# Bias tiles of a two-layer mixer trunk read backwards from reversed rows, without shifted copies in DRAM

## The chip, the core and the metric

The kernel runs on one core of one Trainium2 chip. The metric is the device time of one execution in microseconds (us); a version's time is the median of its runs. The profile shows one execution of the kernel, engine by engine: PE is TensorE, DVE VectorE, ACT ScalarE, POOL GpSimd, and SP the SyncE queue, which here issues nearly all DMAs. Names with a q (SPq) are an engine's instruction queue.

## The reference

Two layers over 512 tokens of width 1024. Each layer normalises x, projects it, runs four attention branches, gates them, projects the outputs back and adds them to x. One table `rel_bias` of 32 buckets and 40 heads gives the relative-position biases of three branches; this is the part that the change touches:

```python
def t5_bucket(dist):                      # distance -> bucket 0..31
    ...
def band_bias(table, step):
    rel = BLOCK + jnp.arange(BLOCK)[:, None] - jnp.arange(2 * BLOCK)[None, :]
    return table[t5_bucket(rel * step)].transpose(2, 0, 1)

# banded_attention (branches B and D): bias (heads, 128, 256), the same for each block of 128 queries
s = jnp.einsum('bnqkgd,bnskd->bnkgqs', qb, kb) * dh ** -0.5
s = s + bias.reshape(hkv, g, BLOCK, 2 * BLOCK)
mask = (rel >= 0)[None] & (rel <= max_dist)[None] & key_ok
s = jnp.where(mask[None, :, None, None], s, -jnp.inf)
# dsa_attention (branch A): the 128 best keys of an indexer
bias = bias_table[t5_bucket(qpos[None, :, None] - idx)]
...
for l in range(DEPTH):
    xn = rms_norm(x, norm_gain[l])
    (A's, B's, C's, D's parts), gates = combined_projection(xn, w_in[l])
    ...
    merged = sum(sigmoid(gates[n]) * ((ys[n] * silu(zs[n])) @ w_branch[l, n]) for n in range(4))
    x = x + merged @ w_out[l]
```

A bias depends on query minus key alone. So the tile of a head, 128 queries by n keys, holds in each row the row above it shifted by one element.

## The kernel before

All products are fp32, made of three TensorE passes over a high and a low part of each operand. A layer runs through a list of jobs (`PLAN`): the indexer; then the branches in the order D, C, B, A, each a row of projection jobs and of attentions, one pair of heads at a time; the merges of a finished branch lie between the jobs of the next; a last group of merges, and the output projection. In the listing `idx`, `cin`, `pair`, `z`, `attD`, `attB` and so on are such jobs. A scheduler of the tile framework, which simulates a timeline, sets the order of each engine's instructions from the jobs' order, from what each needs, and from which buffers are free.

**Weights.** They stream from DRAM (`wall`) through `next_slot`. A slot is loaded by a DMA on SP (L402, `cbuf<-wall`) into one of four raw buffers, ACT casts the high part (L405), DVE subtracts to get the low part (L411), and PE reads both. A load waits on SP for the raw buffer that the subtraction of four slots earlier frees; everything behind it on SP waits with it. SP's DMAs use eight semaphores in turn, so a DMA also waits until the one eight before it has landed.

**Bias rows.** In layer 0 after the indexer, `later_consts` multiplies a one-hot matrix (made on the host by `bias_onehot`: for each position of a segment the bucket of its distance) with the bias table (PE, L335). The result, 41 rows (heads, and one causal row for branch C) by 1920 positions, is written to the DRAM tile `gdram` in four chunks of 480 columns (DVE copy to `th`, then L338). A row holds five segments: A of 640 positions, D 384, and the groups G0 384, G1 256, G2 256 of branch B.

**Shifted copies.** `make_skew` copies a segment of one pair of heads 128 times from `gdram` into another DRAM tile (`skew..`, L347). There are 21 such DMAs: one of 320 KB for C, eight of 384 KB, four of 640 KB and eight of 256 KB, all in layer 0. Their leading dimension is the pair of rows (2), the next the 128 copies with step 0. `load_bias` (L364 to L373) then reads a bias tile on SP (L372) with a step of w - 1 elements per partition, so that the row of partition i is shifted by i. `next_skew` asks for the next copies at certain jobs; `load_bias` does where none are there yet.

**Readers of a bias tile.** DVE adds the bias to the scores and takes the row minimum of the negated sum (L942); for pairs of score parts DVE first adds the bias to the second part (L940, L974); POOL adds the top-k mask in branch A (L934).

**Two other things that the prediction speaks of.** The latent projections of branch C transpose normed rows on PE (L803), from rows `PT` that DVE scales (L796) after ACT has copied a bank of PSUM to `raw` (L642). In branch B the row maxima and denominators of the groups with stride go through a small DRAM tile: `sd<-st` (L1183) and `nat<-sd` (L1185), both on SP, the second waiting for the first to land. PE's L1026 are the products of the probabilities with the values, whose transposed probabilities `PT` come from ACT (L547) and DVE (L548). POOL issues `U<-U` (L701, L702), which swaps halves of the keys.

Of the kernel before, what the change touches and what calls it, by code (L numbers as in the profile page):

```python
# [9 lines left out]
F32 = mybir.dt.float32  # L10
# [6 lines left out]
PSUM = bass.MemoryType.PSUM  # L17
# [5 lines left out]
NT = S // 128  # L23
# [14 lines left out]
SEG_A, SEG_D, SEG_G0, SEG_G1, SEG_G2 = 0, 640, 1024, 1408, 1664  # L38
SEG_LEN = 1920
SEG_ROWS = {SEG_A: (0, 8), SEG_D: (32, 8), SEG_G0: (8, 8), SEG_G1: (16, 8), SEG_G2: (24, 8)}  # L40
# [42 lines left out]
def job_slots(job):  # L83
    """Per weight slot: a list of (source, rows of 128, columns)."""
    kind = job[0]
    if kind in ("idx", "cin", "pair", "d0", "d1"):
        c = chunk_cols(job)
        return [[("w_in", 2 * i + j, c) for j in range(2)] for i in range(4)]
    if kind == "z":
        c = Z_OFF[job[1]] + job[2] * 128 + np.arange(128)  # L90
        return [[("w_in", 4 * i + j, c) for j in range(4)] for i in range(2)]
    if kind == "merge":
        n, ft = job[1], job[2]
        c = OFF_G + n * D + ft * 128 + np.arange(128)
        f = ft * 128 + np.arange(128)
        return [[("w_in", j, c) for j in range(6)],
                [("w_in", j, c) for j in (6, 7)] + [(("w_branch", n), j, f) for j in range(4)]]
    if kind == "out":
        f = job[1] * 128 + np.arange(128)
        return [[("w_out", 4 * i + j, f) for j in range(4)] for i in range(2)]  # L100
    if kind == "cq":
        q = job[1] * 384 + np.arange(384)
        return [[("w_q_b", 0, q), ("w_q_b", 1, q)]]
    if kind == "ckv":
        p = job[1]
        h = np.arange(64)
        kv = np.concatenate([(2 * p) * 128 + h, (2 * p + 1) * 128 + h,
                             (2 * p) * 128 + 64 + h, (2 * p + 1) * 128 + 64 + h])
        return [[("w_kv_b", 0, kv)]]
    raise ValueError(kind)  # L110


def plan():
    """The order of a layer's work; what comes first is preferred where several pieces are ready."""
    w = [("idx",)]
    merges = []

    def fill(n):
        for _ in range(min(n, len(merges))):
            m = merges.pop(0)  # L120
            w.append(m)

    for i, br in enumerate(ORDER):
        n = iter(FILL[i])
        if br == BR_D:
            w += [("d0",), ("d1",)]
            if i < 3 and ORDER[i + 1] == BR_C and CIN_AT < 0:
                w += [("cin",)]
        if br == BR_C and ("cin",) not in w:
            w += [("cin",)]  # L130
        if br == BR_A and ("topk",) not in w:
            w += [("topk",)]
        for p in range(4):
            if br == BR_B:
                for g in range(3):
                    w += [("pair", br, p, g), ("attB", p, g)]
                    if g == Z_AT:
                        w += [("z", br, p)]
                    fill(next(n))
                w += [("mix", p)]  # L140
                continue
            if br == BR_D:
                w += [("z", br, p), ("attD", p)]
            elif br == BR_A:
                w += [("pair", br, p), ("z", br, p), ("attA", p)]
            else:
                if p % 2 == 0:
                    w += [("cq", p // 2)]
                w += [("ckv", p), ("z", br, p), ("attC", p)]
            fill(next(n))  # L150
            w += [("y", br, p)]
            if i < 3 and ORDER[i + 1] == BR_C and p == CIN_AT:
                w += [("cin",)]
        if i < 3:
            merges += [("merge", br, j) for j in range(8)]
    fill(len(merges))
    w += [("merge", ORDER[3], i) for i in range(8)]
    w += [("split",)]
    w += [("out", i) for i in range(8)]
    return w  # L160
# [43 lines left out]
def bias_onehot():  # L204
# [7 lines left out]
    u = np.arange(640)  # L212
    seg(SEG_A, 640, 511 - u, 511 - u >= 0)
    u = np.arange(384)
    seg(SEG_D, 384, 255 - u, (255 - u >= 0) & (255 - u <= 127))
    seg(SEG_G0, 384, 255 - u, (255 - u >= 0) & (255 - u <= 128))
    u = np.arange(256)
# [24 lines left out]
def build(ctx, tc, A, depth=2, dump=None):  # L242
# [68 lines left out]
    skew = {}  # L311
# [28 lines left out]
    def make_skew(seg, r):  # L340
        """Rows r and r + 1 of a segment, 128 copies each, so that a load can shift copy i by i."""
        r0, nr = (C_ROW, 1) if seg == "C" else (SEG_ROWS[seg][0] + r, 2)
        o = SEG_A if seg == "C" else seg
        w = SEG_W[o]
        d = dp.tile([nr, 128, w], F32, name=f"skew{seg}_{r}")
        g = gdram[r0:r0 + nr, o:o + w]
        sy.dma_start(d, bass.AP(tensor=g.tensor, offset=g.offset, ap=[[SEG_LEN, nr], [0, 128], [1, w]]))  # L347
        for i in range(nr):
            skew[seg, r0 + i] = (d[i], w)

    skews = []
    for br in ORDER:
        skews += {BR_A: [(SEG_A, 2 * p) for p in range(4)],
                  BR_B: [(x, 2 * p) for p in range(4) for x in (SEG_G0, SEG_G1, SEG_G2)],
                  BR_C: [("C", 0)],
                  BR_D: [(SEG_D, 2 * p) for p in range(4)]}[br]
    wdma = [None]

    def next_skew():
        """The next segment's copies, behind the weights requested so far."""  # L360
        if skews:
            with tc.issue_after(wdma[0].ins):
                make_skew(*skews.pop(0))

    def load_bias(row, seg, n):
        """[128, n] tile whose row i is the segment's row shifted by i to the right."""
        while (seg, row) not in skew:
            next_skew()
        b = T([128, 512], F32, "bias")[:, :n]
        g, w = skew[seg, row]  # L370
        with tc.issue_after(wdma[0].ins):
            sy.dma_start(b, bass.AP(tensor=g.tensor, offset=g.offset + 127, ap=[[w - 1, 128], [1, n]]))  # L372
        return b  # L373

    def rsqrt(eng, r, ss, n, scale, eps=EPS):
        """r = 1 / sqrt(ss * scale + eps) on [128, n]."""
# [5 lines left out]
    def layer(l, xt):  # L382
# [32 lines left out]
        def gain_parts():  # L415
            """x * gain as hi and lo per row tile: the first products need not wait for the norm."""
# [100 lines left out]
        def t_banks(slots, w, x):  # L517
            """Banks of all token tiles, filled together; x: hi and lo per row tile."""
# [12 lines left out]
        def f_bank(parts, mh, ml, w=S):  # L531
            """parts: (hi, lo) stationary views [128, 128] per row tile; moving operands mh, ml: [128, w] each."""
# [11 lines left out]
        def split_ps(hi, lo, src, scale=None):  # L544
            """hi + lo = src (* scale), src in PSUM."""
# [92 lines left out]
        def evac(o, n, scale=1.0):  # L638
            """A copy of a bank's first n columns, so that the bank is free before the norms are known."""
# [7 lines left out]
        def norm_qk(o, t, x, gi, scale=1.0):  # L647
            """o: two heads of q and of k in PSUM; hi and lo of the normed ones to x[:, t], [128, 4, 2, 64]."""
# [20 lines left out]
        def q_out(uq, qx, hf, h0, n, perm):  # L669
            """Heads of qx [128, 2, n, 2, 64] (half hf of the tokens) to uq[:, h0:h0 + n], feature-major."""  # L670
# [13 lines left out]
        def k_out(kk, x, hf, perm):  # L684
            """The two k heads of x (half hf of the tokens), hi on top of lo, to kk(h, 0)."""
# [12 lines left out]
        def k_swap(kk):  # L698
            """kk(h, 1): lo on top of hi."""
# [83 lines left out]
        def do_cin():  # L783
# [23 lines left out]
            # rotary key, shared by the heads  # L807
# [24 lines left out]
        def do_cq(p, cT):  # L832
            """The normed and rotated queries of two pairs, [128, 2, 4, 96] per half of the tokens."""
# [73 lines left out]
        def scores(kind, step, qk, bias, nm, den, mask, sink, both):  # L907
            """exp of the scores less their maximum, sums to den, minus the maximum to nm."""
# [52 lines left out]
        def attend(kind, qk, v, bias, nm, den, norm, both, mask=None, sink=None):  # L961
            """qk(qb, k0, n): (lhsT, rhs) of the passes; v(kb): stationary [128, 128]; nm/den [128, NT] columns.
            Returns the O bank: rows of V's high part on top of rows of its low part."""
# [73 lines left out]
        def o_sum(dst, o, h, perm):  # L1037
            """Add the halves of an O bank into rows h*64.. of dst, in token order."""
# [109 lines left out]
        for w in PLAN:  # L1148
            kind = w[0]
            if kind == "idx":  # L1150
# [3 lines left out]
                if l == 0:  # L1154
                    later_consts()
                    next_skew()
                    next_skew()
# [3 lines left out]
            elif kind == "z":  # L1161
                szs[w[1:]] = do_z(w[1], w[2])
                if w[1] != BR_C:
                    next_skew()
            elif kind == "pair":
                env["pair"] = do_pair(w)
                if w[1] == BR_B:
                    next_skew()
# [28 lines left out]
            elif kind == "attC":  # L1197
                uq, uk, vv = env["pair"]
                cm = load_bias(C_ROW, "C", 512)
# [24 lines left out]
            elif kind == "d0":  # L1224
                env["d"] = do_d()
                next_skew()
                next_skew()
# [101 lines left out]
```

## Time and profile before

| | us |
|---|---|
| time, three runs | 1955.16, 1951.74, 1954.61 |
| median | 1954.61 |
| span of the profiled execution, first to last instruction | 1949.2 |
| PE busy (97% of the span) | 1884.5 |
| DVE busy (68%) | 1331.1 |
| ACT busy (57%) | 1103.0 |
| POOL busy (37%) | 728.5 |

The profile gives no device time of its own for the execution beside its span; the span stands 5.4 us below the median of the runs. Busy shares say which engine is closest to a bound over the whole span; the waits of an engine and its idle stretches say where that engine stood still and for whom. The chain of waits follows the end of the program back to what released each step.

### The profile page before, as it was taken

The page shows a single profiled execution, that of the slowest core. Times are in us where ns is not written, and L with a number is a line of the kernel's source. Part 1 is how long each engine was busy: PE and PEld are TensorE (multiplying, and loading weights), DVE is VectorE, ACT ScalarE, POOL GpSimd, SP SyncE. Part 2 cuts the span into 40 slices and gives each one's busy share as a digit, 9 for nine tenths or more (in the row PEclk, how much of TensorE's full clock was granted, in tenths as well). Part 3 has the DMA queues.
Part 4 walks back from the last instruction along what each step waited for, and adds up shares of the span by engine and source line. Part 5 has one row for each costly group of instructions (what it writes and reads, how often), then busy time and mean ns, then how long its engine had stood idle before and what let it go on. Part 6 is the DMA issues. An engine that isn't in the chain of part 4 may idle for free.

```text
span 1949.2 us, 33221 instructions
## 1 busy us (share of the span) xinstructions
PE 1884.5 (97%) x11348; PEld 1695.6 (87%) x11348; DVE 1331.1 (68%) x3410; ACT 1103.0 (57%) x2650; POOL 728.5 (37%) x1186
## 2 busy tenths in 40 slices
PE   8759999999989999999999999999999999999999
PEld 7648889989878998998889988899899989898887
DVE  7649777758476866665469888676768686766542
ACT  6538666656455565554347776566555656555431
POOL 3615353424233346640005345253343343755000
PEclk9879999999989999999999999999999999999999
DMA  4223233342334243332252222233333333333233
GB/s 163 84 91 95 67 90 103 105 113 88 110 105 118 80 121 105 99 98 82 91 187 85 82 66 93 74 88 83 94 105 113 101 101 91 117 96 101 80 92 108
DMA packets 103420, 193.47 MB, mean 99 GB/s; under 512 B 21510, under 2 KB 35924, under 8 KB 103252
## 3 DMA queue, kind: packets, MB, share of 16 engines
q1 hardware_dynamic: 92372, 173.52, 29.4%
q0 software_dynamic: 10880, 17.83, 4.2%
q8 instruction: 90, 1.47, 0.3%
q14 instruction: 78, 0.64, 0.1%
HBM read 168.84 MB, written 12.83 MB: 93 GB/s over the span
## 4 chain that ended last, share of the span: by engine, by line
PE 88%; DMA 4%; DVE 2%; ACT 2%; POOL 2%; issue 1%; SPq 1%; DVEq 0%; ACTq 0%; POOLq 0%
PE acc L537 14%; PE acc L536 14%; PE acc L538 14%; PE acc L512 9%; PE acc L513 9%; PE acc L514 9%; PE S L923 4%; PE T L994 3%; PE T L1014 2%; DMA cbuf<-wall 1%; DMA sd<-st 1%; PE T L1033 1%; PE T L1026 1%; PE T L676 1%; PE T L689 1%
## 5 line engine op out<-in xcount | busy, mean ns | idle before, releaser
L411 DVE TENSOR_TENSOR cbufr<-cbuf,cbufr 128x768 fp32r<-128x768 f32 (+3 forms) x396 | 357.6, 906 | 140.5 <-ACT cbufr L405 139.0
L405 ACT CAST cbufr<-cbuf 128x768 fp32r<-128x768 f32 (+3 forms) x396 | 304.9, 774 | 262.4 <-PE acc L537 195.9
L513 PE MATMUL acc<-cbufr 128*128 128x384 f32 (+1 forms) x1152 | 365.8, 318 | 0.0
L512 PE MATMUL acc<-cbufr 128*128 128x384 f32 (+1 forms) x1152 | 364.1, 317 | 0.0
L514 PE MATMUL acc<-cbufr 128*128 128x384 f32 (+1 forms) x1152 | 363.9, 316 | 0.0
L536 PE MATMUL acc<-cbufr 128*128 128x512 f32 x896 | 354.5, 396 | 0.9 <-ACT raw L642 0.9
L538 PE MATMUL acc<-cbufr 128*128 128x512 f32 x896 | 353.9, 395 | 0.0
L537 PE MATMUL acc<-cbufr 128*128 128x512 f32 x896 | 353.6, 395 | 0.0
L513 PEld LDWEIGHTS acc<-cbufr 128*128 128x128 f32 x1152 | 218.7, 190 | 3.0 <-issue 1.1
L512 PEld LDWEIGHTS acc<-cbufr 128*128 128x128 f32 x1152 | 218.5, 190 | 2.7 <-ACT U L696 0.7
L514 PEld LDWEIGHTS acc<-cbufr 128*128 128x128 f32 x1152 | 218.7, 190 | 2.3 <-issue 0.8
L379 POOL TENSOR_TENSOR nr<-nx,cbuf 128x4 f32<-128x4 f32 (+2 forms) x200 | 211.6, 1060 | 11.1
L538 PEld LDWEIGHTS acc<-cbufr 128*128 128x128 f32 x896 | 168.9, 188 | 34.0
L536 PEld LDWEIGHTS acc<-cbufr 128*128 128x128 f32 x896 | 169.0, 189 | 32.7 <-ACT raw L642 1.3
L537 PEld LDWEIGHTS acc<-cbufr 128*128 128x128 f32 x896 | 169.1, 189 | 32.3 <-issue 0.7
L958 POOL TENSOR_SCALAR P<-P,rd 128x128 f32<-128x128 f32 x192 | 117.3, 621 | 195.4 <-DVE rd L956 136.2
L378 POOL TENSOR_SCALAR nx<-nss 128x4 f32<-128x4 f32 (+2 forms) x200 | 62.3, 311 | 272.2 <-DVE nss L653 243.1
L701 POOL DMA_DIRECT2D U<-U x68 | 39.3, 578 | 311.4 <-ACT U L693 190.4
L547 ACT CAST PT<-T 128x128 fp32r<-128x128 f32 (+2 forms) x224 | 102.9, 478 | 64.0 <-PE T L994 38.0
L548 DVE TENSOR_TENSOR PT<-T,PT 128x128 fp32r<-128x128 f32 (+2 forms) x224 | 119.8, 548 | 22.0 <-ACT PT L547 20.3
L945 ACT ACTIVATE P<-P,nm 128x128 f32<-128x128 f32 x192 | 101.9, 533 | 57.4 <-DVE nm L942 56.7
L642 ACT COPY raw<-acc 128x256 f32<-128x256 f32 (+2 forms) x192 | 70.4, 377 | 107.9 <-PE acc L514 74.9
(256 smaller groups left out, 3954.0 us busy)
## 6 DMA issues: line engine op xcount, KB each, us to landing
cbuf<-wall SPq DMA_DIRECT2D x284, 384.0 KB
cbuf<-wall SPq DMA_DIRECT2D x96, 256.0 KB
U<-U POOLq DMA_DIRECT2D x136, 128.0 KB, 2.8
bias<-skew SPq DMA_DIRECT2D x32, 128.0 KB
bias<-skew SPq DMA_DIRECT2D x16, 256.0 KB
skew<-gdram SPq DMA_DIRECT2D x8, 384.0 KB
cbuf<-wall SPq DMA_DIRECT2D x8, 328.0 KB
skew<-gdram SPq DMA_DIRECT2D x4, 640.0 KB
```

Of the source, the lines that this page charges most:

```text
L379: gp.tensor_tensor(r, y, mhalf[:, :n], op=OP.pow)
L405: pin(ac.copy(h, raw))
L411: pin(e.tensor_tensor(lo, raw, h, op=OP.subtract))
L512: mm(o[:, :c1 - c0], x[kt][:, 0, ts], h[:, a + c0:a + c1], start=kt == 0, stop=False)
L513: mm(o[:, :c1 - c0], x[kt][:, 0, ts], lo[:, a + c0:a + c1], start=False, stop=False)
L514: mm(o[:, :c1 - c0], x[kt][:, 1, ts], h[:, a + c0:a + c1], start=False, stop=kt == KT - 1)
L536: mm(o[:, :w], h, mh[kt], start=kt == 0, stop=False)
L537: mm(o[:, :w], h, ml[kt], start=False, stop=False)
L538: mm(o[:, :w], lo, mh[kt], start=False, stop=kt == n - 1)
L547: ac.copy(hi, src)
L548: ve.tensor_tensor(lo, src, hi, op=OP.subtract)
L958: gp.tensor_scalar(p[:, off:off + nk * 128], p[:, off:off + nk * 128], rd[:, qb:qb + 1], 0.0, op0=OP.mult, op1=OP.add)
```

## The change

The host makes the segments of the one-hot matrix in reversed order, so a row of `gdram` runs backwards. `load_bias` reads the bias tile straight from `gdram` with a step of one element per partition and returns it with its columns reversed (`b[:, ::-1]`), so that L942, L940, L974 and L934 read their bias operand with step -1. `make_skew`, `next_skew` and their calls go. The scratch for DMAs that POOL issues is 4096 bytes instead of the default. Comments and docstrings went too, which shifts the line numbers by up to 33 (L402 becomes L377, L372 becomes L345, L338 becomes L337).

```diff
-    u = np.arange(640)
+    u = np.arange(640)[::-1]
     seg(SEG_A, 640, 511 - u, 511 - u >= 0)
-    u = np.arange(384)
+    u = np.arange(384)[::-1]
     seg(SEG_D, 384, 255 - u, (255 - u >= 0) & (255 - u <= 127))
     seg(SEG_G0, 384, 255 - u, (255 - u >= 0) & (255 - u <= 128))
-    u = np.arange(256)
+    u = np.arange(256)[::-1]
...
-    def make_skew(seg, r):
-        r0, nr = (C_ROW, 1) if seg == "C" else (SEG_ROWS[seg][0] + r, 2)
-        o = SEG_A if seg == "C" else seg
-        w = SEG_W[o]
-        d = dp.tile([nr, 128, w], F32, name=f"skew{seg}_{r}")
-        g = gdram[r0:r0 + nr, o:o + w]
-        sy.dma_start(d, bass.AP(tensor=g.tensor, offset=g.offset, ap=[[SEG_LEN, nr], [0, 128], [1, w]]))
...
     def load_bias(row, seg, n):
-        while (seg, row) not in skew:
-            next_skew()
         b = T([128, 512], F32, "bias")[:, :n]
-        g, w = skew[seg, row]
+        g = gdram[row:row + 1, seg:seg + SEG_W[seg]]
         with tc.issue_after(wdma[0].ins):
-            sy.dma_start(b, bass.AP(tensor=g.tensor, offset=g.offset + 127, ap=[[w - 1, 128], [1, n]]))
-        return b
+            sy.dma_start(b, bass.AP(tensor=g.tensor, offset=g.offset + SEG_W[seg] - 127 - n, ap=[[1, 128], [1, n]]))
+        return b[:, ::-1]
...
-    nc = bacc.Bacc("TRN2", target_bir_lowering=False, num_devices=1)
+    nc = bacc.Bacc("TRN2", target_bir_lowering=False, num_devices=1, dynamic_dma_scratch_size=4096)
```

The instructions of PE, ACT and DVE keep their order; on POOL two neighbouring `U<-U` change places once. On SP the 21 copies are gone and bias loads stand earlier. The first place is SP in layer 0 right after the bias rows are made; `gdram<-th` are the four chunks, `cbuf<-wall` weights. Before:

```order
L338 DMA gdram<-th_587 41x480
L402 DMA cbuf<-wall 128x512
L347 DMA skew_0_600<-gdram 256x1x384
L338 DMA gdram<-th_597 41x480
L347 DMA skew_2_602<-gdram 256x1x384
L347 DMA skew_4_1051<-gdram 256x1x384
L402 DMA cbuf<-wall 128x512
L372 DMA bias_1301<-skew_0_600 128x256
L372 DMA bias_1366<-skew_0_600 128x256
L372 DMA bias_1473<-skew_2_602 128x256
L347 DMA skew_6_1053<-gdram 256x1x384
L347 DMA skew_0_1470<-gdram 256x1x384
```

Now:

```order
L337 DMA gdram<-th_587 41x480
L377 DMA cbuf<-wall 128x512
L345 DMA bias_1291<-gdram 128x256
L337 DMA gdram<-th_597 41x480
L345 DMA bias_1356<-gdram 128x256
L345 DMA bias_1461<-gdram 128x256
L377 DMA cbuf<-wall 128x512 x3
L377 DMA cbuf<-wall 128x768
L377 DMA cbuf<-wall 128x256
L377 DMA cbuf<-wall 128x512 x2
```

A bias load stands in the place of the first pair's copies, ahead of the last chunk; the weights that stood behind up to seven copies now follow three bias loads. The second place is SP in layer 0, branch B, around the first `sd` round trip. Before:

```order
L347 DMA skew_4_5127<-gdram 256x1x256
L372 DMA bias_4762<-skew_0_1814 128x128
L402 DMA cbuf<-wall 128x512 x2
L347 DMA skew_4_5269<-gdram 256x1x256
L402 DMA cbuf<-wall 128x768
L372 DMA bias_5134<-skew_2_3974 128x256
L402 DMA cbuf<-wall 128x768
L1183 DMA sd_4460<-st_3976 128x16
L402 DMA cbuf<-wall 128x768
L1185 DMA nat_3977<-sd_4460 128x4x4
```

Now:

```order
L345 DMA bias_4738<-gdram 128x128
L377 DMA cbuf<-wall 128x512 x2
L377 DMA cbuf<-wall 128x768
L345 DMA bias_5108<-gdram 128x256
L377 DMA cbuf<-wall 128x768
L1152 DMA sd_4438<-st_3958 128x16
L377 DMA cbuf<-wall 128x768
L1154 DMA nat_3959<-sd_4438 128x4x4
```

The rows are the same without the copies.

## Rows read from the trace of the kernel before

**Rows 1.** Page: busy time, share of the span, instructions of PE.

```profile
PE 1884.5 (97%) x11348; PEld 1695.6 (87%) x11348; DVE 1331.1 (68%) x3410; ACT 1103.0 (57%) x2650; POOL 728.5 (37%) x1186
```

**Rows 2.** Waits of PE: waiting line, awaited; total us, times, longest.

```profile
PE T L803 <- DVE PT L796: 22.3, 1, 22.3
PE T L1026 <- DVE PT L548: 12.3, 3, 5.2
PE T L676 <- ACT raw L642: 11.7, 1, 11.7
...
PE T L1026 <- ACT PT L547: 3.4, 1, 3.4
```

**Rows 3.** Windows of the span: length, busy PE, PEld, DVE, ACT, POOL (instructions), clock, DMA.

```profile
75.00:150.00 75.00, 41.01 (x220) 36.33 (x219) 32.23 (x99) 27.45 (x72) 19.18 (x41) 0.75 0.30 98
150.00:175.00 25.00, 25.00 (x177) 23.19 (x175) 23.23 (x79) 22.77 (x70) 9.88 (x18) 1.00 0.30 91
...
97.00:101.00 4.00, 4.00 (x14) 3.81 (x14) 2.87 (x8) 3.04 (x7) 1.86 (x4) 0.50 0.13 50
...
137.00:141.00 4.00, 4.00 (x11) 3.30 (x12) 4.00 (x17) 3.60 (x12) 0.00 (x0) 0.50 0.85 287
```

**Rows 4.** Chain of waits, 81 to 136 us: start, length, what.

```profile
81.64 14.50 DMA gdram<-th
...
113.80 7.30 SPq L347
...
121.62 13.52 DMA cbuf<-wall
```

**Rows 5.** Timeline of SP, 85 to 122 us: start, length, line, out<-in, count.

```profile
85.60 11.17 SPq L347 DMA_DIRECT2D skew<-gdram  x2
...
106.03 15.07 SPq L347 DMA_DIRECT2D skew<-gdram  x3
```

**Rows 6.** Line L803 on PE: one instruction's ns, least, median, most.

```profile
L803 PE MATMUL T<-cbuf,PT x16: 270/272/473, 106.3 to 1094.6; 128*128 128x128 f32 x16
```

**Rows 7.** Waits of SP, whole span: the second DMA of the round trip, and a copy.

```profile
SPq L1185 <- DMA sd<-st: 46.5, 16, 9.8
...
SPq L347 <- DMA gdram<-th: 13.2, 2, 7.7
```

**Rows 8.** Waits of SP from 1150 us on, in layer 1.

```profile
SPq L1185 <- DMA sd<-st: 12.2, 8, 2.3
```

**Rows 9.** Chain of waits, the mix of branch B in either layer (transposes L1135).

```profile
437.11 0.89 PE S L1135 x3
...
490.23 9.47 DMA sd<-st
...
554.16 0.89 PE S L1135 x3
...
1388.72 0.89 PE S L1135 x3
...
1488.52 0.89 PE S L1135 x3
```

**Rows 10.** Timeline of PE, 390 to 396 us: in brackets the idle time before.

```profile
395.62 0.57 PE L1026 MATMUL T<-PT,U 128*64 128x128 f32 x6 [2.58 <-DVE PT L548]
```

**Rows 11.** The tile named bias: one instruction's ns, least, median, most; start times; forms.

```profile
L942 DVE CUSTOM_DVE_ANT_0 P<-S,bias x128: 272/418/691, 205.6 to 1812.0; 128x256 f32<-128x256 f32 x64, 128x128 f32<-128x128 f32 x32, 128x384 f32<-128x384 f32 x16, 128x512 f32<-128x512 f32 x16
L372 SPq DMA_DIRECT2D bias<-skew x80: 320/384/4321, 104.6 to 1761.3; - x80
L942 DVE CUSTOM_DVE_ANT_0 P<-S,bias,cbuf x64: 323/473/484, 137.0 to 1129.3; 128x256 f32<-128x256 f32 x48, 128x128 f32<-128x128 f32 x16
L974 DVE TENSOR_TENSOR bm<-S,bias x64: 400/411/425, 373.0 to 1665.3; 128x256 f32<-128x256 f32 x64
L934 POOL TENSOR_TENSOR bm<-bias,cbuf x48: 664/1102/1702, 730.6 to 1800.3; 128x256 f32<-128x256 f32 x16, 128x384 f32<-128x384 f32 x16, 128x512 f32<-128x512 f32 x16
```

**Rows 12.** Page: DMA issues of POOL, KB each, us from issue to landing.

```profile
U<-U POOLq DMA_DIRECT2D x136, 128.0 KB, 2.8
```

More of the change, by code (lines that the diff above doesn't have):

```diff
@@ L36 @@
 Z_OFF = (OFF_A + 1536, OFF_B + 4608, OFF_C + 416, OFF_D + 768)
-SEG_A, SEG_D, SEG_G0, SEG_G1, SEG_G2 = 0, 640, 1024, 1408, 1664
+SEG_A = SEG_C = 0
+SEG_D, SEG_G0, SEG_G1, SEG_G2 = 640, 1024, 1408, 1664
 SEG_LEN = 1920
-SEG_ROWS = {SEG_A: (0, 8), SEG_D: (32, 8), SEG_G0: (8, 8), SEG_G1: (16, 8), SEG_G2: (24, 8)}
 SEG_W = {SEG_A: 640, SEG_D: 384, SEG_G0: 384, SEG_G1: 256, SEG_G2: 256}
@@ L310, in build @@
     gdram = dp.tile([C_ROW + 1, SEG_LEN], F32, name="gdram")
-    skew = {}
     def late_consts():
@@ L338, in later_consts, with load_bias @@
             sy.dma_start(gdram[:, i * 480:(i + 1) * 480], gs)
-    def make_skew(seg, r):
-        r0, nr = (C_ROW, 1) if seg == "C" else (SEG_ROWS[seg][0] + r, 2)
-        o = SEG_A if seg == "C" else seg
-        w = SEG_W[o]
-        d = dp.tile([nr, 128, w], F32, name=f"skew{seg}_{r}")
-        g = gdram[r0:r0 + nr, o:o + w]
-        sy.dma_start(d, bass.AP(tensor=g.tensor, offset=g.offset, ap=[[SEG_LEN, nr], [0, 128], [1, w]]))
[L348 to L356, printed above, removed]
-    wdma = [None]
[L359 to L365, printed above, removed]
-        while (seg, row) not in skew:
-            next_skew()
-        b = T([128, 512], F32, "bias")[:, :n]
-        g, w = skew[seg, row]
-        with tc.issue_after(wdma[0].ins):
-            sy.dma_start(b, bass.AP(tensor=g.tensor, offset=g.offset + 127, ap=[[w - 1, 128], [1, n]]))
-        return b
+    def load_bias(row, seg, n):
+        b = T([128, 512], F32, "bias")[:, :n]
+        g = gdram[row:row + 1, seg:seg + SEG_W[seg]]
+        with tc.issue_after(wdma[0].ins):
+            sy.dma_start(b, bass.AP(tensor=g.tensor, offset=g.offset + SEG_W[seg] - 127 - n, ap=[[1, 128], [1, n]]))
+        return b[:, ::-1]
+    wdma = [None]
     def rsqrt(eng, r, ss, n, scale, eps=EPS):
@@ L1155, in layer @@
                     later_consts()
-                    next_skew()
-                    next_skew()
             elif kind == "topk":
@@ L1162, in layer @@
                 szs[w[1:]] = do_z(w[1], w[2])
-                if w[1] != BR_C:
-                    next_skew()
             elif kind == "pair":
                 env["pair"] = do_pair(w)
-                if w[1] == BR_B:
-                    next_skew()
             elif kind == "attB":
@@ L1198, in layer @@
                 uq, uk, vv = env["pair"]
-                cm = load_bias(C_ROW, "C", 512)
+                cm = load_bias(C_ROW, SEG_C, 512)
                 ss[BR_C, w[1]] = s = T([128, 512], F32, "s")
@@ L1225, in layer @@
                 env["d"] = do_d()
-                next_skew()
-                next_skew()
             elif kind == "attD":
```

## The prediction

> **What bounds the kernel now.** The first view is the busy shares: PE is busy for 1884.5 of 1949.2 us [rows 1]. So the kernel is bound by its products, and at most some 65 us can be gained by removing idle time. The second view is the list of PE's waits, which shows where this idle time lies: it is not spread, four entries hold 49.7 us of it (22.3 + 12.3 + 11.7 + 3.4) [rows 2]. The question for this change is who made PE wait there, and for each entry I followed the chain of waits back.
>
> The entry of 11.7 us is L676 waiting for ACT's copy `raw` (L642). The chain shows that this copy itself stood for the landing of a chunk of bias rows, 14.50 us from 81.64 us on [rows 4]. SP was sending copies meanwhile: two of them took 11.17 us of the queue [rows 5]. The entry of 22.3 us is L803 waiting for DVE. The chain leads through SP, which was held by a copy for 7.30 us, to a weight load that took 13.52 us to land [rows 4]; the three copies in front of that load took 15.07 us of SP's queue together [rows 5]. So both waits come from the DMAs that make shifted copies: once as a full queue in front of weights, once as bytes of which the later transfers stand behind. The window shows the result: PE is busy for 41.01 of 75 us, and its clock is granted at 0.75; in the 25 us behind it, with PE busy throughout, at 1.00 [rows 3].
>
> The other 15.7 us (12.3 + 3.4, L1026) lie in branch B. There the chain shows PE waiting, through DVE, for the `sd` round trip: one `sd` DMA of 8 KB took 9.47 us [rows 9]. SP's waits give the whole: in 16 trips the second DMA waited 46.5 us for the first, at most 9.8; the eight trips of layer 1 account for 12.2 of that, at most 2.3 [rows 7, 8]. The difference between the layers in that part is that only layer 0 makes copies. This comparison carries much of my sum: layer 1 is layer 0 without copies, and none of the four waits occurs in it.
>
> **The change part by part.** *Front of layer 0.* Without the copies SP has no 11.17 and 15.07 us of them in front of the weights [rows 5]. I take both waits as gone: 11.7 + 22.3 = 34.0 us [rows 2]. To that comes the clock. After each of the two gaps PE ran for a while at half its clock, 1.2 GHz instead of 2.4: the windows at 97 and at 137 us are fully busy at 0.50 [rows 3]. Either window lies within a slow stretch, which I read as 9 us busy for both (4.00 + 4.00 plus about 1 at the edges). The same transpose takes 473 ns at the low and 272 at the usual level [rows 6], so 9 us become 9 x 272 / 473 = 5.2: 3.8 us more. What is late next there? The last chunk now stands behind a bias load that waits for the chunk before it; copies waited so too, 13.2 us in two waits, at most 7.7 [rows 7]. Behind that bias load wait the last chunk and three weights. ACT's copy `raw` no longer carries the wait for the last chunk: another placement of buffers gives it to a later instruction of ACT. I allow 3.5 us of new idle time here, near the low end of the bounds 0 and 14.5 (the landing of [rows 4] unchanged), since most of that landing was spent beside copies and none are left.
>
> *Branch B of layer 0.* From the first to the last of the two marks (the transposes of the mix) layer 0 takes 554.16 - 437.11 = 117.05 us, layer 1 for the same work 1488.52 - 1388.72 = 99.80 [rows 9]. The 17.25 us between them are the waits of that stretch with their clock. One earlier wait of the same kind, 2.58 us, lies ahead of the first mark [rows 10]. I take all 19.8 us as gain, since layer 1 has the bias loads and weights of the same stages and no such wait. Bounds: 10, if the round trips keep half their length, and 22.
>
> *Bias loads.* They are as many as before and have the same size, so SP issues them at the same 0.384 us each [rows 11]. What is new is their source: 128 overlapping rows out of one row of `gdram`, instead of 128 different rows. The trace of before shows no such load into SBUF. In layer 1 the loads have some 950 us to spare and are asked for ahead of their readers, so I take 0; bounds are 0 and 88 x 7.3 us (a copy's hold, [rows 4]) of SP's queue, of which the waiting weights would hide most.
>
> *Reading backwards.* By medians the bias readers take 128 x 0.418 + 64 x 0.473 + 64 x 0.411 = 110 us on DVE and 48 x 1.1 = 53 on POOL [rows 11]. No row shows a step of -1. The nearest is L974: its bias operand, 128 elements read twice by a step of 0, is no plain run either, and its 256 elements take 411 ns, no more than L942's median of 418 [rows 11]. So I take 0; bounds are -0 (no reason for a gain) and, at twice the price, +110 on DVE and +53 on POOL, of which only what reaches PE counts.
>
> The Trainium skill speaks to this. "Vector Engine (DVE) Microarchitecture Reference", section 5.1, lists an operand with a negative step as not measured. "GPSIMD Engine Reference", section 7, prices reads whose step is above 8 bytes at half as much again; 4 bytes backwards are not named there. By its price, as an estimate, POOL's 53 us would become 80, and PE would wait for none of it unless branch A's POOL became late.
>
> *The rest.* 21 DMA issues less on SP, the reversed segments and the comments cost nothing: the one-hot product has the same shape, and SP waits for DVE most of its time. The smaller scratch concerns POOL's `U<-U`; 136 of them land in 2.8 us each [rows 12], spread over the span, so I take 0; it would cost if POOL had to wait for room, at most 2.8 us a time.
>
> **The sum** is 34.0 + 3.8 + 19.8 - 3.5 = 54.1 us. 1949.2 - 54.1 = 1895.1 us of span. The median of the runs stands 5.4 us above the span of the profiled execution, so the forecast is 1900.5, say 1900 us.
>
> **The rivals.** *Part of the front stays.* The chunks of bias rows are made and sent as before, and the first bias load waits on SP with the weights behind it. If the landing of the last chunk stays at 14.5 us, the wait of 11.7 us stays, and half of 22.3 with it: 1900 + 11.7 + 11 - 3.5, about 1919. For it speaks that a chunk's DMA took up to 7.7 us to land even before most copies were sent [rows 7]; against it, that the weights are asked for early and the three copies between are gone. By the Trainium skill, "DMA: Bandwidth & Descriptors", section "Why a DMA increments its semaphore by 16 and not by 1", a transfer uses as many engines, up to 16, as divide its slowest dimension: 2 for the copies' leading pair, 16 for 128 partitions, but one for the chunks' 41 rows. The trace agrees as to the copies, which held SP 7.30 us [rows 4]; by the rule the bias loads would not, and the chunks would remain slow, which is this rival.
>
> *The direct loads are slow.* If 128 rows out of the same 1 to 2.5 KB land as late as the copies did, each load delays the weights and the `sd` trips around it, now in both layers. Only the excess over 34 + 20 us would make it slower; I price it as the 19.8 us of branch B staying in layer 0 and coming up in layer 1 as well, less 20%: 1900 + 32 = 1932.
>
> *Backward reads cost, and the kernel is slower.* The place is every attention. In the stretch of branch D's attention DVE is busy for 23.23 of 25 us [rows 3], so nearly all that is added there reaches PE. At twice the price, 163 us in sum on both engines, slower begins where more than 54 us, a third of it, reach the path. With half of it: 1900 + 81 = 1981. Against it speaks L974; for it, that nothing in the trace shows the step.
>
> *Nothing gained.* The copies only happened to be in flight, and the chunks and the 8 KB trips are slow by themselves: 1955. Layer 1, whose trips wait 12.2 us in all, speaks against it [rows 8].
>
> **How the numbers follow.** Forecast 0.70, own range 1890 to 1912 (the front's bounds and branch B's); front stays 0.13; slow loads 0.05; nothing gained 0.04; backward reads 0.08. The range runs from 1889 to 1931: it takes in the forecast, the front and most of the slow loads. This kernel's runs tell a difference of about 0.2% from none. Faster by more: 0.70 + 0.13 + 0.05 = 0.88; within it 0.04; slower 0.08.
>
> **What would show it.** In the profile after, PE's waits should hold neither L803 nor L676 with more than 4 us, and those of L1026 under 2 in all. The window 75 to 150 us should have PE busy for over 70 us and the clock near 1. SP's wait for `sd` should be near 25 us over the whole span, with no single one above 3. The two marks of branch B should be 100 us apart in both layers. L942 and L974 should keep medians of 418, 473 and 411 ns, POOL's reader 1102; a rise there is the last rival's sign. A wait of ACT for a chunk of bias rows at 80 to 95 us is the first rival's. A new wait of SP behind bias loads in layer 1, which is undisturbed now, would be the second's. I would be wrong altogether if the two layers' waits still differed.

## The result, and the profile after

The changed kernel takes 1893.42 us (median; 1892.81 to 1894.28), the kernel before 1954.09 in the same comparison (1951.74 to 1955.16). The ratio is 0.9692, with a 95% interval of 0.9678 to 0.9706: 3.1% faster. The forecast was 1900 us, own range 1890 to 1912, so its direction and likeliest case held and it was 6.6 us too long.

The page of the changed kernel begins with the span and the busy time of each engine, and its row of the granted clock (in tenths of full speed, 40 slices) has a 9, so 90% or more, in each:

```profile
span 1892.5 us, 33118 instructions
PE 1875.0 (99%) x11348; PEld 1688.0 (89%) x11348; DVE 1334.9 (71%) x3410; ACT 1103.4 (58%) x2650; POOL 732.4 (39%) x1186
...
PEclk9999999999999999999999999999999999999999
```

The span is 56.7 us shorter than before (1949.2). PE's busy time fell by 9.5 us [rows 1] although it does the same 11348 products: that is the part that came from the clock. (Taken over windows of 1 us, busy time times what the granted clock lacked of 1 comes to 4.8 us before 160 us and 4.5 between 437 and 560 us in the kernel before, and to 0 now.) The other 47.2 us are idle time. What is left of PE's waits (awaited line; total us, times, longest):

```profile
PE acc L501 <- ACT cbufr L380: 6.3, 1, 6.3
PE acc L502 <- DVE cbufr L386: 2.0, 1, 2.0
PE acc L488 <- DVE cbufr L386: 1.9, 1, 1.9
PE T L778 <- DVE PT L771: 1.8, 2, 1.0
```

The first stands at the program's start in both kernels, and the next two before 34 us, ahead of all that the change touches. Of the four waits of [rows 2], three are gone, and the one of 22.3 us (L803, now L778) is 1.8. The windows of the front (length; busy PE, PEld, DVE, ACT, POOL with instructions; clock, DMA share, GB/s):

```profile
75.00:150.00 75.00, 72.72 (x460) 65.55 (x459) 64.86 (x205) 59.78 (x168) 38.58 (x71) 1.00 0.34 86
```

Before, the same 75 us held 220 products and 41.01 us of busy PE at a clock of 0.75 [rows 3]; now 460 and 72.72 at 1.00. The marks of branch B's mix, from the chain of waits (start, length, what), first in layer 0, then in layer 1:

```profile
399.18 0.89 PE S L1110 x3
...
498.97 0.89 PE S L1110 x3
...
1333.29 0.89 PE S L1110 x3
...
1433.09 0.89 PE S L1110 x3
```

They are 99.79 us apart in layer 0 and 99.80 in layer 1, where before it was 117.05 and 99.80 [rows 9]. The two layers now take the same time. SP's waits that answer to [rows 7] (waiting line, awaited; total us, times, longest):

```profile
SPq L1154 <- DMA sd<-st: 26.5, 16, 3.4
...
SPq L345 <- DMA gdram<-th: 7.0, 1, 7.0
```

The `sd` trips cost SP 26.5 us over both layers where it was 46.5, and the longest is 3.4 (forecast: near 25, none above 3). The second row is a wait that the copies had before: the first bias load still stands 7.0 us on SP for a chunk of bias rows. ACT, which waited 15.4 us for the last chunk before, waits for no chunk now; DVE does:

```profile
DVE qn L749 <- DMA gdram<-th: 3.8, 1, 3.8
```

Last, the tile named bias (one instruction's ns, least, median, most; start times; forms), which answers to [rows 11]:

```profile
L917 DVE CUSTOM_DVE_ANT_0 P<-S,bias x128: 273/419/692, 171.4 to 1755.0; 128x256 f32<-128x256 f32 x64, 128x128 f32<-128x128 f32 x32, 128x384 f32<-128x384 f32 x16, 128x512 f32<-128x512 f32 x16
L345 SPq DMA_DIRECT2D bias<-gdram x88: 320/423/1682, 79.3 to 1708.6; - x88
L917 DVE CUSTOM_DVE_ANT_0 P<-S,bias,cbuf x64: 328/474/486, 104.9 to 1073.7; 128x256 f32<-128x256 f32 x48, 128x128 f32<-128x128 f32 x16
L949 DVE TENSOR_TENSOR bm<-S,bias x64: 401/414/429, 337.9 to 1609.9; 128x256 f32<-128x256 f32 x64
L909 POOL TENSOR_TENSOR bm<-bias,cbuf x48: 666/1110/1705, 675.3 to 1743.3; 128x256 f32<-128x256 f32 x16, 128x384 f32<-128x384 f32 x16, 128x512 f32<-128x512 f32 x16
...
DMA to landing us min/median/max: 2.8/3.4/5.8
```

The readers' medians are 419, 474, 414 and 1110 ns, where they were 418, 473, 411 and 1102 [rows 11]. A bias load takes SP 423 ns where it took 384. The direct loads land in 3.4 us at the median.

### The profile page after: what moved, and what is told of

Read it like the earlier page. It is cut to its first block, busy times and chain, and to the rows that moved or that the text cites. A ratio compares the mean times of both kernels' runs of the same rounds, so it can differ in the third digit from the quotient of the medians.

```text
span 1892.5 us, 33118 instructions
## 1 busy us (share of the span) xinstructions
PE 1875.0 (99%) x11348; PEld 1688.0 (89%) x11348; DVE 1334.9 (71%) x3410; ACT 1103.4 (58%) x2650; POOL 732.4 (39%) x1186
## 4 chain that ended last, share of the span: by engine, by line
PE 96%; DVE 1%; POOL 1%; DMA 1%; ACT 1%; issue 0%; SPq 0%; DVEq 0%; ACTq 0%; POOLq 0%
PE acc L513 15%; PE acc L512 15%; PE acc L511 15%; PE acc L487 10%; PE acc L488 10%; PE acc L489 10%; PE S L898 4%; PE T L969 4%; PE T L989 2%; PE T L1008 1%; PE T L651 1%; PE T L1001 1%; PE T L664 1%; DMA cbuf<-wall 1%; PE S L946 1%; PE T L870 1%
## 5 line engine op out<-in xcount | busy, mean ns | idle before, releaser
L676 POOL DMA_DIRECT2D U<-U x68 | 38.9, 572 | 291.1 <-ACT U L668 182.7
```

## The experiments

The theory was that the copies cost by their form, and not by being needed: SP's queue was held behind them, and transfers issued after them landed late. Rivals were their volume, the bias loads' wait for them, and the order of instructions. Experiments e1 and e2 are built on the opposite sides: one keeps copies and readers and changes the form, the other keeps the form and takes away the readers.

**Copies in another form (e1).** The kernel before, with

```diff
-        sy.dma_start(d, bass.AP(tensor=g.tensor, offset=g.offset, ap=[[SEG_LEN, nr], [0, 128], [1, w]]))
+        sy.dma_start(d.rearrange("r p w -> p r w"),
+                     bass.AP(tensor=g.tensor, offset=g.offset, ap=[[0, 128], [SEG_LEN, nr], [1, w]]))
```

> The kernel before, with one edit: each copy DMA has the 128 copies as its outermost dimension and the pair of rows inside, so that the same bytes go to the same places in DRAM. The theory (it is the form of the copies that cost: few transfer engines, each busy for long, SP's queue held and weights landing behind) expects most of the gain without dropping a byte: PE's waits at L803 and L676 under 5 us each, the longest wait for sd under 4 us, 1895 to 1910 us. The rival (the 8 MB written and read again cost by their volume) expects 1945 to 1955 us, with the waits where they were. A second rival (the bias loads' wait for copies costs, whatever their form) expects 1925 to 1950.

It took 1901.26 us; ratio to before 0.9739 (0.9725 to 0.9754). So 52 us of the change's 60 come without dropping a byte. SP's timeline (start, length, line, out<-in, count) and PE's wait:

```profile
80.66 0.58 SPq L347 DMA_DIRECT2D skew<-gdram  x1
...
81.80 1.20 SPq L347 DMA_DIRECT2D skew<-gdram  x2
...
90.93 1.86 SPq L347 DMA_DIRECT2D skew<-gdram  x3
```

```profile
PE T L677 <- ACT raw L643: 5.5, 1, 5.5
...
PE T L1027 <- DVE PT L549: 1.5, 2, 1.0
```

The two and three copies that held SP for 11.17 and 15.07 us [rows 5] now take 1.20 and 1.86. The wait at L803 is gone, that at L676 fell from 11.7 to 5.5 (expected: under 5), and branch B's from 15.7 to 1.5; the longest wait for `sd` is 5.0 (expected: under 4). The volume is not the main cost. The order of instructions is not either: by the trace every engine and SP have the same order here as before.

**Copies that nobody reads (e2).** The kernel before with the reversed rows and the changed `load_bias`, so that the 21 copies go out at their old jobs in their old form but have no reader:

```diff
-        g, w = skew[seg, row]
+        o = SEG_A if seg == "C" else seg
+        g = gdram[row:row + 1, o:o + SEG_W[o]]
         with tc.issue_after(wdma[0].ins):
-            sy.dma_start(b, bass.AP(tensor=g.tensor, offset=g.offset + 127, ap=[[w - 1, 128], [1, n]]))
-        return b
+            sy.dma_start(b, bass.AP(tensor=g.tensor, offset=g.offset + SEG_W[o] - 127 - n, ap=[[1, 128], [1, n]]))
+        return b[:, ::-1]
```

> The changed kernel with the 21 copies put back at their old jobs, in their old form, but read by nobody: bias tiles still come straight from the reversed rows and are read backwards. The theory expects the loss back, 1940 to 1955 us, with PE waits at the lines of L803 and in branch B as before (22 and 15 us) since SP and the transfers behind it are held as before. The rival (what cost was that bias loads had to wait for copies to land) expects 1893 to 1900 us, since nobody waits for these copies.

It took 1955.6 us; ratio 1.0015 (1.0005 to 1.0025): the whole gain is gone again. SP's timeline, the chain behind it, then PE's waits:

```profile
84.31 37.30 SPq L347 DMA_DIRECT2D skew<-gdram  x6
```

```profile
121.72 13.94 DMA cbuf<-wall
```

```profile
PE T L804 <- DVE PT L797: 31.2, 1, 31.2
PE T L1027 <- DVE PT L549: 13.1, 3, 5.1
...
PE T L677 <- ACT raw L643: 3.5, 1, 3.5
PE T L1027 <- ACT PT L548: 3.4, 1, 3.4
```

Six copies in a row hold SP's queue for 37.30 us, with the weights behind them. In the front, PE waits 34.7 us (31.2 + 3.5), where it was 34.0, and in branch B 16.5 us (13.1 + 3.4), where it was 15.7. That bias loads had to wait for copies is therefore not the cause. Nor are the reversed rows and the backward reads in themselves the gain: they are in this kernel too. (This kernel, e5, e6 and e8 keep the default scratch; e11 prices that.)

**Reading forwards (e3).** The changed kernel with `return b` in place of `return b[:, ::-1]`.

> The changed kernel with the bias tiles read forwards; the biases are then added in reversed column order, so this leaves out the reversal and its output is not the reference's. Backward reads cost nothing by the theory: 1893 us within 0.2%, and the DVE readers' medians stay at 419, 474 and 414 ns, POOL's at 1110 ns. The rival (a step of -1 costs something that the gain hides) expects lower medians on DVE or POOL, 5% or more, and 1885 to 1890 us.

It took 1893.73 us, against 1893.42 with the reversal; ratio to before 0.9696 (0.9682 to 0.9711). The readers:

```profile
L917 DVE CUSTOM_DVE_ANT_0 P<-S,bias,cbuf x64: 326/471/484, 105.3 to 1073.9; 128x256 f32<-128x256 f32 x48, 128x128 f32<-128x128 f32 x16
L949 DVE TENSOR_TENSOR bm<-S,bias x64: 400/411/425, 338.2 to 1610.0; 128x256 f32<-128x256 f32 x64
L909 POOL TENSOR_TENSOR bm<-bias,cbuf x48: 662/1100/1327, 675.6 to 1743.2; 128x256 f32<-128x256 f32 x16, 128x384 f32<-128x384 f32 x16, 128x512 f32<-128x512 f32 x16
```

Forwards against backwards the medians are 471 and 474, 411 and 414, 1100 and 1110 ns. The difference is under 1% on both engines, and none of it reaches the time.

**Copies on POOL's queue (e4).** The kernel before with `gp.dma_start` for the copies, and the changed kernel's scratch.

> The kernel before, with its 21 copies in their old form issued by POOL instead of SP (and the changed kernel's scratch for POOL's DMAs, as the default one leaves too little room). It tells apart two ways in which the copies cost. If SP's held queue was the cost, weights go out on time and the time is 1893 to 1912 us. If the cost is that few transfer engines are busy for long and other transfers' shares land behind them, SP being free changes little: weight loads still land late, PE waits over 10 us at L803 or L676 and over 10 us in branch B, 1930 to 1955 us. I expect something between, nearer to the second, about 1930; POOL's own issue time (some 1 us each) is no matter, as POOL is busy for 37%.

It took 2093.48 us; ratio 1.072 (1.0704 to 1.0736). My estimate of 1930 was far off, because I held POOL's part for 1 us a copy. POOL's waits, PE's, and the copies' time to land (KB each, median us):

```profile
POOL skew L347 <- issue: 188.2, 19, 19.2
```

```profile
PE T L676 <- DVE qk L777: 127.8, 4, 98.5
```

```profile
skew<-gdram POOLq DMA_DIRECT2D x8, 384.0 KB, 10.8
```

POOL stood 188.2 us before 19 of its copies, with its norms behind it, for which DVE and then PE waited. SP stood 90.1 us for the copies that its bias loads read. The issue itself is the 1 us that I had assumed; but from the third on POOL issues a copy only when the one before has landed (at 127.59 us for instance, after a landing at 127.28). Whether the queue or the small scratch makes it wait was not tested. PE, DVE and ACT also got another order of instructions in this run, so its time is no price of the queue alone. It did not separate a held queue from slow transfers.

**By place (e5, e6).** The kernel of e2 with a condition on `make_skew`'s DMA, so that only some copies are made; e5 has the condition shown, e6 its opposite:

```diff
+        if seg in ("C", SEG_D) or (seg in (SEG_G0, SEG_G1, SEG_G2) and r == 0):
```

> The changed kernel with eight of the 21 copies put back, unread and in their old form: C's, the four of D and the first of each group of B, which all fall into the first 150 us. The theory adds up by place: the front's loss comes back (34.7 us of idle time in the run with all copies unread, and some 4 of clock), branch B's does not: 1930 to 1936 us, PE's waits in branch B under 2 us. The rival (copies cost by their number, wherever they stand) expects 8/21 of 62 us, 1917.

> The changed kernel with the other 13 copies put back, unread and in their old form: the remaining ones of B and those of A, which go out one at a time from 340 us on and hold SP for 0.6 us each. Theory: here SP's queue is not held, but the sd round trips land behind the copies' bytes on few transfer engines, so branch B's loss comes back alone: 1911 to 1917 us, some 16 us of PE's waits in branch B and none over 3 us before 150 us. If only a held queue costs, 1894 to 1897.

With the early ones it took 1930.7 us (ratio 0.9888, 0.9874 to 0.9903), with the late ones 1917.9 (0.9822, 0.9807 to 0.9836); the second is 0.9 over what was expected. Against 1893.42 these are 37.3 and 24.5 us, 61.8 together, and all copies unread cost 62.2 (1955.6). So the loss adds up by place, not by number: eight copies cost 37.3, thirteen 24.5. Beside the changed kernel the order of SP differs by the added copies alone, and that of PE, DVE and ACT not at all. PE's waits with the early ones, then with the late ones:

```profile
PE T L807 <- DVE PT L800: 31.1, 1, 31.1
...
PE T L680 <- ACT raw L646: 3.5, 1, 3.5
```

```profile
PE T L1030 <- DVE PT L552: 13.3, 3, 5.1
...
PE T L1030 <- ACT PT L551: 3.7, 1, 3.7
```

In e6 the copies go out singly. SP's timeline shows one, then the `sd` trip that follows it, and the chain shows how long that trip's first DMA took:

```profile
485.67 0.60 SPq L350 DMA_DIRECT2D skew<-gdram  x1
487.02 5.60 SPq L406 DMA_DIRECT2D cbuf<-wall  x2
...
494.30 0.70 SPq L1187 DMA_DIRECT2D sd<-st  x1
504.76 0.38 SPq L1189 DMA_DIRECT2D nat<-sd  x1
```

```profile
494.30 10.45 DMA sd<-st
```

The copy holds SP for 0.60 us. The first load of weights behind it holds SP for 4.81 of the 5.60 us, but that is over at 491.8 us and not on the chain. Then 8 KB issued behind the copy, after three loads of weights and a bias load, take 10.45 us to land; in the changed kernel `sd` lands in 2.8 us at the median. So in branch B the cost is not a held queue but a transfer that lands late.

**Chunks of 48 rows (e7, e10), and the changed kernel beside it (e9).** The first bias load's wait of 7.0 us was left over. In e7 the rows are padded from 41 to 48:

```diff
-    gdram = dp.tile([C_ROW + 1, SEG_LEN], F32, name="gdram")
+    gdram = dp.tile([48, SEG_LEN], F32, name="gdram")
...
-                mm(o[:C_ROW + 1, :480], rhl[:, e], ohr, start=e == 0, stop=e == 1)
-            gs = T([128, 512], F32, "th")[:C_ROW + 1, :480]
-            ve.tensor_copy(gs, o[:C_ROW + 1, :480])
+                mm(o[:48, :480], rhl[:, e], ohr, start=e == 0, stop=e == 1)
+            gs = T([128, 512], F32, "th")[:48, :480]
+            ve.tensor_copy(gs, o[:48, :480])
```

> The changed kernel with the bias rows padded from 41 to 48, so that a chunk's DMA writes 48 rows. If 41 rows go over one transfer engine and 48 over 16, a chunk lands in 2 to 4 us where the wait of SP's first bias load on it was 7.0; bias loads and the weights behind them go out some 4 us earlier, and what is left of PE's waits in that stretch (1.8 us) may go: 1891 to 1893.5 us. If the number of rows is of no matter, the wait stays near 7 and the time at 1893.4.

> The changed kernel itself, unedited, beside the next two on one chip, so that small differences can be told: 1893.4 us, within 0.1%.

> The changed kernel with chunks of 48 rows, again, on the same chip as the changed kernel. If its first run was more than luck, it takes 1.5 to 3.5 us less than the changed kernel here, since 3.1 us of PE's idle time (13.4 to 10.3 us) are gone from its profile; if not, within 1 us of it.

It took 1890.8 us the first time, 0.2 below the expected range (ratio to before 0.9682, 0.9667 to 0.9696). On one chip with the changed kernel it took 1890.31 (1890.07 to 1890.81) and that 1893.06 (1892.39 to 1893.8): 2.75 us less, and the ranges do not meet. The intervals of their ratios to the kernel before, 0.9659 to 0.9686 and 0.9673 to 0.9699, do meet, since that kernel scatters by 6 us itself. SP's wait in e7, and how long its four chunks took to land:

```profile
SPq L346 <- DMA gdram<-th: 0.9, 1, 0.9
```

```profile
DMA to landing us min/median/max: 1.9/2.8/3.6
```

The wait fell from 7.0 to 0.9 us by seven more rows, and the waits at L778 (here L779) disappeared from PE's list. This is the fastest version of the study. The Trainium skill, "DMA: Bandwidth & Descriptors", section "Why a DMA increments its semaphore by 16 and not by 1", has a transfer's slowest dimension decide on how many engines it runs: 1 for 41 rows and 16 for 48, 2 for the copies before and 16 for those of e1. The traces agree with it, also in the number: the increments of the DMAs' semaphores, in the table behind e12, are 1, 16, 2 and 16.

**Spread copies that nobody reads (e8).** The kernel of e2 with the form of e1.

> The changed kernel with all 21 copies put back unread, in the form with the 128 copies outermost. The run with these copies read took 1901.3 us. If its 7.8 us over the changed kernel came from bias loads waiting for copies to land, this takes 1893 to 1896; if from the copies' bytes as such, 1899 to 1903 again.

It took 1900.66 us; ratio 0.9734 (0.9718 to 0.975), in the range of the second alternative: the copies cost 7 us even in the better form, with no reader. SP's timeline, PE's waits and the wait behind the first of them:

```profile
83.15 7.94 SPq L347 DMA_DIRECT2D skew<-gdram  x6
```

```profile
PE T L678 <- ACT raw L644: 3.5, 1, 3.5
PE T L1028 <- DVE PT L550: 2.3, 2, 1.4
```

```profile
ACT raw L644 <- DMA gdram<-th: 7.3, 1, 7.3
```

That the bytes cost is not shown, though. At L678 PE waits for the last chunk of bias rows, with a stretch at the low clock behind it. C's copy, which reads the first chunks, waits for one of them on SP, and the last two chunks behind it go out later: the last at 81.06 us, where e11, without copies, sends it at 77.59. So part of the 7 us seems to come from a copy that waits in the queue; how much, was not tested. The same 3.5 us stand in the lists of e2 and e5.

**The scratch (e11).** The changed kernel without `dynamic_dma_scratch_size=4096`.

> The changed kernel with one part undone, the smaller scratch for POOL's DMAs. The theory holds this part for worth nothing: within 1 us of the changed kernel. A rival by which the small scratch makes POOL wait for room expects 2 us less or better; one by which it helps (buffers elsewhere, other waits) expects 2 us more.

It took 1893.91 us (1892.6 to 1894.75) beside 1893.06 of e9: no difference, as expected.

**Two copies in the front (e12).** As e5, with the condition `seg == SEG_D and r in (0, 2)` and the changed kernel's scratch.

> The changed kernel with only two of the 21 copies put back, the first two of D, unread, in their old form, in the front stretch. With six in a row SP's queue was held for 37.3 us there; two should go out at 0.6 us each, as single copies do in branch B, so this takes the held queue away and leaves the bytes. If what cost in the front is mostly the held queue, PE loses under 3 us: 1893 to 1896. If it is also that weight loads land behind the copies' bytes, as the sd trips do in branch B, weights land 5 to 15 us late and PE waits 5 to 15 us at L803: 1899 to 1910.

It took 1897.18 us; ratio 0.9713 (0.9697 to 0.9729). Its premise failed. SP's timeline and PE's wait:

```profile
81.11 8.05 SPq L350 DMA_DIRECT2D skew<-gdram  x2
```

```profile
PE T L807 <- DVE PT L800: 3.8, 2, 3.0
```

The second of two copies was held, the two for 8.05 us in sum. So the run did not take the held queue away, and its time lies between the two alternatives. But the hold is not on the chain that ends in PE's wait. There SP waits for a free buffer until 96.83 us, and then this load of weights lands late:

```profile
96.85 8.15 DMA cbuf<-wall
```

So the first 8 us of a hold hide, and what PE waited here was a late landing.

**When the shares of a transfer land (from the kept traces).** The trace keeps the time of every increment of a DMA's semaphore, which no view prints. Those at the landing, in us:

| transfer | issued | increments when it lands |
|---|---|---|
| copy in the old form, e2 | 98.78 | 2: 120.06, 121.73 |
| copy in e1's form | 81.80 | 16: 87.48 to 90.55 |
| chunk of 41 rows, changed kernel | 79.71 | 1: 85.24 |
| chunk of 48 rows, e7 | 72.83 | 16: 74.36 to 75.54 |
| `sd`, kernel before | 490.23 | 14: 492.61 to 494.14; 499.44, 499.69 |
| `sd` behind a copy, e6 | 494.30 | 14: 497.31 to 498.38; 504.52, 504.74 |
| weights behind two copies, e12 | 96.85 | 14: 99.18 to 99.48; 103.11, 104.99 |
| weights behind six copies, e2 | 121.72 | 14: 131.79 to 132.43; 133.99, 135.66 |

I call a share what one of these increments closes. A copy in the old form has two (C's, of a single row, has 16), and of the transfers behind such copies two of sixteen are late. The DMA share of the windows fits: 0.13 while copies are on their way [rows 3], which is two of sixteen engines. So a late landing is two shares that stand behind the copies' two.

The last row also divides the front's wait of 31.2 us in e2, which begins at 106.3 us. Until 121.6 the copies hold SP's queue, and the load of weights itself is held there for another 8.05 us, to 129.8; 14 shares have landed by 132.4, the last two 3.2 us later, and ACT, DVE and PE need the rest. So the front's cost with copies in a row is for the most part the held queue (23.5 us), and late shares are 3.2 us of it.

## Why the prediction held, point by point

**Front of layer 0.** Forecast: 34.0 us of idle time and 3.8 of clock gone, 3.5 new, 34.3 in sum. At the first mark of branch B the changed kernel is 437.11 - 399.18 = 37.93 us ahead [rows 9]. The forecast to that point was 34.3 + 2.58 = 36.9. Shown by e5: the early copies alone bring 37.3 us back. The new idle time that I allowed came out at 1.8 us instead of 3.5, and the clock at 4.8 instead of 3.8. The reason that I gave for the small allowance was wrong: SP's wait for the chunk is still 7.0 us without copies, since the chunk has one share only, but the weights behind it have most of that to spare; e7, which removes that wait, gains 2.75 us. One reading was off as well: the weight load of 13.52 us [rows 4] was not late by all of that. SP's queue was held for 7.64 us of them at the load itself.

**Branch B.** Forecast 19.8 us. Of the gain, 17.26 lie between the marks: the lead grows from 37.93 to 554.16 - 498.97 = 55.19 us [rows 9]. The other 2.58 was the wait ahead of the first mark, which is gone. Taking layer 1 as the model of layer 0 without copies was exact: 99.79 and 99.80 us. What the prediction took for the cause, the bytes ahead of the `sd` trips, is shown by e6 and by the late shares.

**Bias loads and backward reads.** Both were taken at 0, and PE pays nothing for either. The loads land in 3.2, 4.1 and 3.5 us (64, 128 and 256 KB, medians of the DMA list) where the loads from 128 different rows in e1 took 2.8, 3.5 and 3.4, so up to 0.6 us later, and no wait of PE leads to one. Backwards, e3 has the same time and readers' medians within 1%. This term had bounds up to +163 us, since no row of before showed a step of -1. The experiment closes them for this kernel.

**The scratch and the 21 issues.** Taken at 0; e11 agrees for the scratch.

**Where it was off.** The sum gave a span of 1895.1 us and it is 1892.5: 2.6 too long, as much as the front's allowance (1.7) and its clock (1.0) together; differences elsewhere cancel (the start of the program, ahead of the change, was 2.2 us slower in this execution). The other 4 us are the last step, from span to time. I added 5.4 us, the distance of the one profiled execution from the median of the runs. In the runs of this study the profiled execution's own time stands 1.8 to 2.1 us above its span, for instance 1894.28 beside 1892.5. By that measure the profiled execution of before took about 1951, at the low edge of its kernel's runs; some 3.5 of the 5.4 us were chance and did not belong to the changed kernel. The runs of before spread over 1950.27 to 1956.9 us, those of the changed kernel over 1892.39 to 1894.28. So a part of the scatter seems to have gone with the copies as well. What in them scatters is open: e1 and e8, with spread copies, scatter by 5.9 and 5.3 us too.

**The rivals.** That part of the front stays: its sign, a wait of ACT for a chunk, is absent, but the chunks are slow as it said (7.0 us on SP, 3.8 on DVE). They are nearly off the path: e7 puts their price at 2.75 us, where the rival had 19. Slow direct loads, costly backward reads and no gain at all are excluded by the landing times, by e3 and by e2.

## What to carry to other kernels

Ask of a DMA not only what it moves but how many rows its outermost dimension has: the same bytes with 128 rows outside instead of 2 gave 52 of the 60 us here, and 48 rows instead of 41 gave 2.75. A transfer that nobody on the critical path reads can still set the time, through the queue that issues it and through what is issued behind it; so follow a late landing back to the transfers ahead of it. Where a program repeats a stage without the suspect, as layer 1 does here, the difference of the two stages is the best price to be had before a change.

## What the runs showed that was not expected

Copies without a reader cost as much as copies with one (62.2 against 60.7 us). Even spread, and unread, they cost 7 us. A queue on POOL was no refuge: POOL stood 188.2 us before 19 of them. Behind a copy, 14 of 16 shares of an 8 KB transfer landed in time and the last two 5 to 6 us later. And seven unused rows in a 77 KB write shortened the wait for it from 7.0 to 0.9 us.
